# Weight splitter of a three-product fp32 block: a 60-unit ring of blocks becomes 15 equal cells, two kinds of VectorE additions become adding transfers, two preparations are spread out

## The chip, the cores and the metric

One core of one Trainium2 chip runs the whole kernel. The metric is the device time of one execution in microseconds; what is given is the median of several runs. TensorE, VectorE, ScalarE, GpSimd and SyncE are PE, DVE, ACT, POOL and SP in the profile's rows, and PEld is TensorE's loading of weights.

## The reference, cut to what matters

The input `x` has 256 tokens of 4096 channels. It is normalized, projected to 20480 channels, mixed in two branches, gated, merged and projected back; the residual is added, and a last RMSNorm follows.

```python
h = rmsnorm(x, norm_w)
proj = einsum('bsd,de->bse', h, w_in)              # 4096 -> 20480
u_p, z_p, u_c, b_c, c_c, z_c, g_logit = split(proj)
y_pool = causal_multiscale_pool(u_p, pool_w, pool_scale) * silu(z_p)   # windows 2, 4, 8, 16
y_conv = causal_gated_shortconv(u_c, b_c, c_c, conv_w, conv_b) * silu(z_c)
br = einsum('bsnc,ncd->bsnd', stack([y_pool, y_conv], 2), w_branch)    # 2 x (2048 -> 4096)
merged = sum(sigmoid(g_logit + gate_b) * br, axis=2)
x = x + einsum('bsd,de->bse', merged, w_out)       # 4096 -> 4096
return rmsnorm(x, final_norm_w)
```

## The kernel before

**Numbers.** Every fp32 operand of a product is split in two parts: ACT writes the rounded part (`act` to a float32r tile, the "high"), DVE writes what is left (`sub`, the "low"). A product is then three matmuls: high by high, high by low, low by high.

**Units and steps.** The work is a list of 32 units, each a block of 1024 output columns for all 256 tokens: 8 of the convolution (`cz`, `cb`, `cu`, `cc` for c = 0, 1), 4 of the pooling (`pz`, `pu`), 8 gate units (`g0_0`, `g1_0`, ... `g1_3`), 8 branch units (`b0_0` ... `b1_3`) and 4 output units (`o0` ... `o3`). A unit goes through its rows of weights in steps of 256 rows by 1024 columns (1 MB), 16 steps for 4096 rows and 8 for 2048. A string such as `EIGHT = "PSPSPSPSPSPSPSPS"` or `SIX4 = "PPPPSPSPSPSPSPSP"` gives the kind of each step. A **P** step multiplies directly: 24 matmuls of 128x512. An **S** step uses a seven-product scheme: 21 matmuls, but four sums of weight quarters must be formed first. In steps of both kinds TensorE streams the split weights and holds the split activations, which lie in `arena`.

**From weight to product.** SP loads a step's 1 MB into one of three `raw` buffers. For P, ACT writes highs of 2048 columns and DVE the lows. For S, ACT writes three quarters' highs, DVE forms four sums in `sums` (profile: `parts`), ACT writes their highs, DVE writes both kinds of lows. All go to `ring`, a tile of 60 units of 256 columns. `Ring.alloc` looks for a contiguous free block: 16 units for P, 12 for the three quarters of S, 16 for its sums, 16 or 8 for other uses. `Ring.release` gives a P block back in two halves, after 12 matmuls each, and an S block product by product.

**Order.** Every instruction is recorded in program order and engines follow that order. `pump()` lays preparation (`first()`, `rest()` of each step, in a queue `work`, first in, first out) up to four steps ahead of the step being multiplied, whenever the ring has room. `tick()` runs once per six matmuls and takes one entry from `queue`, a unit's epilogue; `gap(n)` puts n empty entries in it. `pop_fill()`, also once per tick, splits stored activations for the branch and output units. At a unit's end `combine(u)` adds the seven-product scheme's corner terms to the unit's result on DVE. The result stands in `E`, or in `Y` for some.

**Epilogues that matter here.** A gate unit adds a bias row to `E` on DVE: before its end POOL loads the row, broadcast to 128 partitions, into `Y`; then `add(E, E, ...)`, a sigmoid on ACT, a store. An output unit adds the residual rows of `x`, one token half at a time, through `Y`. `make_bands(c)` builds the banded matrices of the pooling on POOL and DVE, in one piece at the start of `cb0` and of `pu1`. In the first unit, `cz0`, `x_operand(j)` prepares x for step j just ahead of that step; for an S step that is two ACT scalings into `sa`, four DVE sums, an ACT high and a DVE low of 896 or 1024 columns.

Of the kernel before, what the change touches and what calls it, by code (L numbers as in the profile page):

```python
# [26 lines left out]
RING = 60  # L27
# [17 lines left out]
def hybrid_block(ctx: ExitStack, tc: tile.TileContext, x, xc, prm, rows_in, w_in, pool_w, w_branch, w_out, out):  # L45
# [28 lines left out]

    const = ctx.enter_context(tc.tile_pool(name="const", bufs=1))
# [8 lines left out]
    ring = sb("ring", [P, RING * KB], F32R)  # L84
# [67 lines left out]
    class Block:  # L152
        def __init__(self, at, parts):
            self.at, self.parts = at, parts

    class Ring:
        def __init__(self, size):
            self.size, self.head, self.live = size, 0, []

        def alloc(self, n, unit):  # L160
            for at in list(range(self.head, self.size - n + 1, 4)) + list(range(0, min(self.head, self.size - n + 1), 4)):
                if all(at >= a + m or a >= at + n for a, m in self.live):
                    parts = [(at + i, unit) for i in range(0, n, unit)]
                    self.live += parts
                    self.head = at + n
                    return Block(at, parts)
            return None

        def release(self, part):
            self.live.remove(part)  # L170

    rg = Ring(RING)

    def piece(block, off, n):
        o = (block.at + off) * KB
        return ring[:, o:o + n * KB]

    class Step:
        def __init__(self, unit, kind, src=None, op=None, **kw):
            self.unit, self.kind, self.src, self.op = unit, kind, src, op  # L180
            self.__dict__.update(kw)
            self.raw = None
            self.prepared = False
            self.pre = []

        def first(self):
            if self.kind == "P":
                def halves(block):
                    v = piece(block, 0, 16).rearrange("p (n a k c) -> p n a k c", n=2, a=2, k=2)
                    self.h, self.l, self.block = v[:, :, 0], v[:, :, 1], block  # L190
                    self.q = self.raw.rearrange("p (k n c) -> p n k c", k=2, n=2)
                    self.ks = (slice(0, 1), slice(1, 2)) if self is steps[0] else (slice(0, 2),)
                    for ks in self.ks:
                        act(self.h[:, :, ks], self.q[:, :, ks])

                return [((16, 8), None, halves)]
            if self.kind == "S":
                def direct(block):
                    self.q = self.raw.rearrange("p (i n) -> p i n", i=4)
                    self.bd = block  # L200
                    self.dh, self.dl = self.split(block, 3)
                    act(self.dh, self.q[:, 0:3])

                return [((12, 4), None, direct)]
            if self.kind == "M":
                def weights(block):
                    self.bw = block
                    self.h = piece(block, 0, 8).rearrange("p (k n) -> p k n", k=4)
                    self.l = piece(block, 8, 8).rearrange("p (k n) -> p k n", k=4)
                    self.q = self.raw.rearrange("p (k n) -> p k n", k=4)  # L210
                    act(self.h, self.q)

                return [((16, 16), None, weights)]
            return []

        def split(self, block, n):
            v = piece(block, 0, 4 * n).rearrange("p (i a n) -> p i a n", i=n, a=2)
            return v[:, :, 0], v[:, :, 1]

        def rest(self):  # L220
            if self.kind == "P":
                def lows(_):
                    for ks in self.ks:
                        sub(self.l[:, :, ks], self.q[:, :, ks], self.h[:, :, ks].bitcast(F32))

                return [(None, None, lows)]
            if self.kind == "S":
                def added(block):
                    q = self.q
                    self.bt = block  # L230
                    self.th, self.tl = self.split(block, 4)
                    add(sums[:, 0:2], q[:, 3:4].to_broadcast([P, 2, NH]), q[:, 1:3])
                    act(self.th[:, 0:2], sums[:, 0:2])
                    add(sums[:, 2], sums[:, 0], q[:, 2])
                    add(sums[:, 3], sums[:, 2], q[:, 0])
                    act(self.th[:, 2:4], sums[:, 2:4])
                    sub(self.dl, q[:, 0:3], self.dh.bitcast(F32))
                    sub(self.tl, sums, self.th.bitcast(F32))

                return [((16, 4), None, added)]  # L240
            if self.kind == "B":
                def parts(block):
                    self.block = block
                    self.h = piece(block, 0, 8).rearrange("p (t n) -> p t n", t=2)
                    self.l = piece(block, 8, 8).rearrange("p (t n) -> p t n", t=2)
                    act(self.h, E)
                    sub(self.l, E, self.h.bitcast(F32))

                return [((16, 16), lambda: self.unit.flags.get("base"), parts)]
            g = self.g  # L250
            e = E.rearrange("p a n -> p (a n)")[:, g * 1024:(g + 1) * 1024].rearrange("p (k t) -> p k t", k=4)

            def lows(_):
                sub(self.l, self.q, self.h.bitcast(F32))

            def pooled(block):
                self.ba = block
                self.ah = piece(block, 0, 4).rearrange("p (k t) -> p k t", k=4)
                self.al = piece(block, 4, 4).rearrange("p (k t) -> p k t", k=4)
                act(self.ah, e)  # L260
                sub(self.al, e, self.ah.bitcast(F32))

            return [(None, None, lows), ((8, 8), lambda: self.unit.flags.get(f"pooled{g}"), pooled)]

        def groups(self):
            gs = []
            if self is steps[0]:
                for k in (1, 0):
                    for i in range(3):
                        for n in range(2):  # L270
                            for t in range(2):
                                ah, al = self.op.standing(k, t)
                                h, l = self.h[:, 1 - n, 1 - k], self.l[:, 1 - n, 1 - k]
                                gs.append([("E", t, n), [((ah, h), (al, h), (ah, l))[i]], ()])
                gs[-1][2] = self.block.parts
            elif self.kind == "P":
                for n in reversed(self.halves):
                    for t in self.toks:
                        mm = []
                        for k in range(2):  # L280
                            ah, al = self.op.standing(k, t)
                            h, l = self.h[:, 1 - n, 1 - k], self.l[:, 1 - n, 1 - k]
                            mm += [(ah, h), (ah, l), (al, h)]
                        gs.append([("E", t, n), mm, ()])
                    if self.final:
                        gs[-1][2] = self.block.parts[1 - n:2 - n]
# [759 lines left out]
```

## Time and profile before

| | |
|---|---|
| median of 3 runs | 2499.02 us (2497.69 to 2499.75) |
| profiled execution: its own time | 2499.66 us |
| profiled execution: span of the trace | 2498.0 us |
| PE, DVE, ACT, POOL busy, share of the span | 96%, 87%, 57%, 3% |
| DMA, mean over the span | 220 GB/s |
| packets' share of the 16 DMA engines: SP's queue, POOL's queue | 53.8%, 7.1% |

The page first gives each engine's busy time, then the span in 40 slices, the DMA queues, the chain that ended last, and the costliest groups of instructions. A group's row has the line, the engine, the operation, output and inputs with shapes, the count, the busy time and the mean of one, and after the second bar the engine's idle time just before these instructions with what ended it. A timeline's row gives start and length in us and, in brackets, the idle time before it. A line such as L55 is a helper's (`tt`), so groups are told apart by their tiles.

### The profile page before, as it was taken

The numbers are of one execution on the slowest core, as the hardware profiler recorded it, in microseconds if no ns is written. First come the engines' busy times: TensorE is split into PE (matmuls) and PEld (weight loads), VectorE is DVE, ScalarE is ACT, GpSimd is POOL, SyncE is SP. The second block draws the span as 40 slices with busy tenths as digits, with TensorE's granted clock in tenths as the row PEclk, the third lists the DMA queues.
The fourth block names the chain that finished last, engine by engine and source line by source line (L and its number), as shares of the span: only waits on it lengthen the run. The fifth ranks groups of instructions, "written<-read, shape, count | busy, mean of one in ns | idle before, by whom it ended". The sixth has DMA issues, their size and how long they took to land.

```text
span 2498.0 us, 26581 instructions
## 1 busy us (share of the span) xinstructions
PE 2402.2 (96%) x10497; PEld 1963.3 (79%) x10497; DVE 2175.5 (87%) x1680; ACT 1417.8 (57%) x1294; POOL 66.5 (3%) x142
## 2 busy tenths in 40 slices
PE   8899999999999999999999999999999999999998
PEld 6677887888878888788777877887788877778886
DVE  7888899889988969869988998898888789899998
ACT  6655555555555546546555555555565555556555
POOL 0000000000000000000000000000000001000000
PEclk9899999999999999999999999999999999999999
DMA  8455466556556645546655665576767757557657
GB/s 305 167 202 202 165 239 212 194 201 227 196 198 217 218 174 203 203 176 219 238 210 188 232 240 206 186 260 219 248 230 271 267 216 276 210 185 279 229 212 274
DMA packets 82062, 549.15 MB, mean 220 GB/s; under 512 B 9360, under 2 KB 9360, under 8 KB 19856
## 3 DMA queue, kind: packets, MB, share of 16 engines
q1 hardware_dynamic: 68832, 484.47, 53.8%
q0 software_dynamic: 12672, 61.87, 7.1%
q8 instruction: 82, 1.34, 0.2%
q10 hardware_dynamic: 432, 1.11, 0.1%
q14 instruction: 44, 0.36, 0.0%
HBM read 518.05 MB, written 29.36 MB: 219 GB/s over the span
## 4 chain that ended last, share of the span: by engine, by line
PE 37%; DVE 13%; ACT 5%; issue 3%; DMA 0%; DVEq 0%; ACTq 0%
PE sums L857 29%; PE shared L857 7%; DVE ring L55 6%; ACT ring L52 3%; DVE parts L55 2%; DVE raw L55 1%; DVE E L55 1%; ACT E L52 1%; ACT raw L52 1%; DVE arena L55 1%; PE shared L541 0%; DMA raw<-in_w_out_dram 0%; DVE E L67 0%; ACT arena L52 0%; PE shared L388 0%
## 5 line engine op out<-in xcount | busy, mean ns | idle before, releaser
L857 PE MATMUL sums<-ring,arena 128*128 128x512 f32 x7827 | 1855.2, 394 | 69.9 <-DVE ring L55 51.3
L857 PEld LDWEIGHTS sums<-ring,arena 128*128 128x128 f32 x7827 | 1477.7, 190 | 401.4 <-DVE ring L55 72.2
L55 DVE TENSOR_TENSOR ring<-raw,ring 128x1536 fp32r<-128x1536 f32 (+2 forms) x453 | 929.8, 2053 | 188.1 <-ACT ring L52 173.2
L52 ACT ACTIVATE ring<-raw 128x1536 fp32r<-128x1536 f32 (+2 forms) x453 | 780.5, 1728 | 463.1 <-PE sums L857 296.4
L52 ACT ACTIVATE ring<-parts 128x1024 fp32r<-128x1024 f32 x390 | 407.0, 1060 | 349.4 <-DVE parts L55 325.8
L857 PE MATMUL shared<-ring,arena 128*128 128x512 f32 x2340 | 568.0, 391 | 0.6 <-DVE Y L67 0.4
L857 PEld LDWEIGHTS shared<-ring,arena 128*128 128x128 f32 x2340 | 439.9, 189 | 97.9 <-DVE ring L55 5.5
L55 DVE TENSOR_TENSOR ring<-parts,ring 128x2048 fp32r<-128x2048 f32 x195 | 445.9, 2287 | 47.2 <-ACT ring L52 42.8
L55 DVE TENSOR_TENSOR parts<-parts,raw 128x512 f32<-128x512 f32 x390 | 269.9, 692 | 13.3
L55 DVE TENSOR_TENSOR parts<-raw 128x1024 f32<-128x1024 f32 x195 | 237.7, 1219 | 2.8 <-DMA raw<-in_w_in_dram 1.3
L55 DVE TENSOR_TENSOR raw<-raw 128x512 f32<-128x512 f32 (+1 forms) x93 | 80.6, 867 | 2.1
L52 ACT ACTIVATE raw<-shared 128x512 f32<-128x512 f32 x124 | 68.5, 625 | 7.3 <-DVE ring L55 7.3
L52 ACT ACTIVATE E<-sums,rin 128x512 f32<-128x512 f32 x56 | 35.6, 689 | 51.6 <-PE sums L857 51.6
L55 DVE TENSOR_TENSOR E<-E,Y 128x2048 f32<-128x2048 f32 (+1 forms) x29 | 60.0, 2068 | 3.3 <-DMA Y<-p_d 3.0
L52 ACT ACTIVATE arena<-sa 128x512 fp32r<-128x512 f32 (+2 forms) x28 | 22.1, 790 | 54.1 <-DVE sa L55 48.5
L52 ACT ACTIVATE E<-sums 128x512 f32<-128x512 f32 x44 | 23.8, 598 | 36.7 <-PE sums L857 36.7
L55 DVE TENSOR_TENSOR arena<-sa,arena 128x512 fp32r<-128x512 f32 (+2 forms) x28 | 24.9, 890 | 19.6 <-ACT arena L52 19.5
L67 DVE SCALAR_TENSOR_TENSOR E<-raw,rin,E 128x1024 f32<-128x1024 f32 x28 | 34.7, 1282 | 0.6
L388 PE MATMUL shared<-ident,E 128*128 128x128 f32 x128 | 18.9, 282 | 10.6 <-DVE E L55 10.6
L388 PEld LDWEIGHTS shared<-ident,E 128*128 128x128 f32 x128 | 15.8, 146 | 14.9 <-issue 12.2
L55 DVE TENSOR_TENSOR E<-E,raw 128x2048 f32<-128x2048 f32 x11 | 25.2, 2292 | 0.4
L52 ACT ACTIVATE E<-E 128x2048 f32<-128x2048 f32 (+1 forms) x12 | 19.4, 1619 | 5.0 <-DVE E L55 5.0
(110 smaller groups left out, 387.9 us busy)
## 6 DMA issues: line engine op xcount, KB each, us to landing
raw<-in_w_in_dram SPq DMA_DIRECT2D x319, 1024.0 KB, 4.8
raw<-in_w_branch_dram SPq DMA_DIRECT2D x64, 1024.0 KB, 5.8
raw<-in_w_out_dram SPq DMA_DIRECT2D x64, 1024.0 KB, 4.9
gates_d<-E POOLq DMA_DIRECT2D x8, 1024.0 KB, 6.4
Y<-gates_d POOLq DMA_DIRECT2D x8, 1024.0 KB, 6.6
Y<-in_rows_dram POOLq DMA_DIRECT2D x12, 512.0 KB, 7.6
Y<-in_xc_dram SPq DMA_DIRECT2D x16, 256.0 KB, 5.7
E<-in_x_dram POOLq DMA_DIRECT2D x4, 1024.0 KB, 5.5
```

What stands on the lines that cost most here:

```text
L52: return pin(nc.scalar.activation(dst, src, func, **kw))
L55: return pin(nc.vector.tensor_tensor(out=dst, in0=a, in1=b, op=op))
L67: return pin(nc.vector.scalar_tensor_tensor(out=dst, in0=a, scalar=s, in1=b, op0=op0, op1=op1, **kw))
L388: pin(nc.tensor.transpose(shared(j)[:, i * T + t * P:i * T + (t + 1) * P], src[:, t, c:c + P], ident))
L857: pin(nc.tensor.matmul(ps, lhs, rhs, start=n == 0, stop=n == u.total[b] - 1))
```

## The change

The ring becomes 15 cells, each with a high and a low of 512 columns (the same memory). `alloc` takes the next n cells in circular order, which need not be contiguous; every cell is given back by itself. A run of cells that wraps round the end of the ring is written by two instructions in place of one. A P step's matmuls go by weight quarter (k outside n), so that a cell is free after six matmuls. An S step's sums and its direct lows are recorded before its four sum cells are asked for. Gate biases and the output's residual rows are added to `E` by POOL-issued transfers that accumulate, two per unit. The bands are built in timed pieces in the epilogues of `cu0` and `pz1`. x's sums have a second stage buffer, and their scaling, sums and lows are put in different steps. Some gaps and the sigmoid's and SiLU's pieces change.

```diff
-RING = 60
+CELLS = 15
+    def gather(dst, src):
+        return pin(nc.gpsimd.dma_start(dst, src, accum_op=ALU.add))
...
-    ring = sb("ring", [P, RING * KB], F32R)
+    ring = sb("ring", [P, CELLS, 2, NH], F32R)
...
+        def alloc(self, n):
+            cells = [(self.head + i) % CELLS for i in range(n)]
+            if self.live & set(cells):
+                return None
+            self.live |= set(cells)
+            self.head = (self.head + n) % CELLS
+            return cells
...
+    def highs(cells, src):
+        for i, c in runs(cells):
+            act(ring[:, c, 0], src[:, i])
+    def lows(cells, src):
+        for i, c in runs(cells):
+            sub(ring[:, c, 1], src[:, i], ring[:, c, 0].bitcast(F32))
...
             if self.kind == "S":
-                def added(block):
+                def added(_):
                     q = self.q
                     add(sums[:, 0:2], q[:, 3:4].to_broadcast([P, 2, NH]), q[:, 1:3])
-                    act(self.th[:, 0:2], sums[:, 0:2])
                     add(sums[:, 2], sums[:, 0], q[:, 2])
                     add(sums[:, 3], sums[:, 2], q[:, 0])
-                    act(self.th[:, 2:4], sums[:, 2:4])
-                    sub(self.dl, q[:, 0:3], self.dh.bitcast(F32))
-                    sub(self.tl, sums, self.th.bitcast(F32))
-                return [((16, 4), None, added)]
+                    lows(self.cells, q[:, 0:3])
+                def split(cells):
+                    self.sum_cells = cells
+                    highs(cells[0:2], sums[:, 0:2])
+                    highs(cells[2:4], sums[:, 2:4])
+                    lows(cells, sums)
+                return [(None, None, added)] + self.mid + [(4, None, split)]
...
             elif self.kind == "P":
-                for n in reversed(self.halves):
-                    for t in self.toks:
-                        for k in range(2):
...
-                    if self.final:
-                        gs[-1][2] = self.block.parts[1 - n:2 - n]
+                for k in (1, 0):
+                    for n in reversed(self.halves):
+                        cell = self.cells[2 * (1 - k) + 1 - n]
+                        for t in self.toks:
+                            ah, al = self.op.standing(k, t)
+                            gs.append([("E", t, n), [(ah, high(cell)), (ah, low(cell)), (al, high(cell))], ()])
+                        if self.final:
+                            gs[-1][2] = [cell]
...
     def gate_unit(n, c):
-        def start():
-            move(Y[:, 0], gate_b[n, None, c * NU:(c + 1) * NU].to_broadcast([P, NU]))
         def epi(u):
-            return gap(2) + [lambda: add(E, E, Y[:, 0:1].to_broadcast([P, 2, NU]))] + gap(3) + [
-                lambda: act(E, E, AF.Sigmoid), lambda: move(gates_d[n, c], E)]
+            def bias(t):
+                gather(E[:, t], gate_b[n, None, c * NU:(c + 1) * NU].to_broadcast([P, NU]))
+            return gap(1) + [lambda: bias(0), lambda: bias(1)] + gap(12) + [
+                lambda: act(E[:, 0], E[:, 0], AF.Sigmoid), None,
+                lambda: act(E[:, 1], E[:, 1], AF.Sigmoid), lambda: move(gates_d[n, c], E)]
...
-            return gap(1) + [lambda: mul(E, E, Y), lambda: move(Y, p_d[c])] + gap(7) + [
-                lambda: add(E, E, Y)] + gap(4) + pairs(transposes(E, copy)) + [
+            return gap(1) + [lambda: mul(E, E, Y), lambda: move(Y, p_d[c])] + gap(9) + [
+                lambda: add(E, E, Y)] + gap(5) + pairs(transposes(E, copy)) + [
...
             def row(t):
-                move(Y[:, 1], xrows[:, t, cs])
+                gather(E[:, t], xrows[:, t, cs])
...
-            return [lambda: row(0)] + gap(8) + [lambda: add(E[:, 0], E[:, 0], Y[:, 1]), lambda: row(1)] + gap(8) + [
-                lambda: add(E[:, 1], E[:, 1], Y[:, 1])] + gap(2) + [
+            return gap(1) + [lambda: row(0), lambda: row(1)] + gap(14) + [
                 lambda: square(0), lambda: square(1),
...
+        return [trailing] + gap(4) + [counts, leading] + gap(4) + [finished]      # band_items(c)
...
+    for j in range(16):
+        if j in staged:
+            steps[j - 1].pre.append(item(x_scale, j))
+            steps[j - 1].mid.append(item(x_sums, j))
+            steps[j].mid.append(item(x_rest, j))
         else:
-            parts_of(o, sa[:, 0:o.n])
+            before(j, x_direct, j)
...
-            make_bands(0)
-        if u.name == "pu1":
-            make_bands(1)
```

`x_scale` is the two ACT scalings, `x_sums` the four DVE sums with the ACT high, `x_rest` the DVE low; `x_direct` is the P steps' old path. `band_items(0)` stands in the epilogue of `cu0`, `band_items(1)` in that of `pz1`.

More of the change, by code (lines that the diff above doesn't have):

```diff
@@ L183, in __init__ @@
             self.prepared = False
-            self.pre = []
+            self.pre, self.mid = [], []
         def first(self):
[L187 to L218, printed above, removed]
+            if self.kind == "B":
+                return []
+            def rounded(cells):
+                self.q = self.raw.rearrange("p (i c) -> p i c", i=4)
+                self.cells = cells
+                if self is steps[0]:
+                    for i in (slice(0, 2), slice(2, 4)):
+                        highs(cells[i], self.q[:, i])
+                else:
+                    highs(cells, self.q[:, 0:len(cells)])
@@ L512, in band_sums, with finished @@
+        def finished():
+            for g in range(2):
+                w, q = WINDOWS[2 * c + g], scratch(g)
+                stt(edge[:, g], ident, -float(w), q[:, 0:P], ALU.mult, ALU.add)
+                stt(bands[:, g, 0:P], ident, cnt[:, g:g + 1], q[:, 0:P], ALU.mult, ALU.add)
+                pin(nc.vector.tensor_copy(bands[:, g, P:T], q[:, P:T]))
+        return [trailing] + gap(4) + [counts, leading] + gap(4) + [finished]
     def band_sums(st):
```

242 lines of the change are left out of this document (128 added, 114 removed).

## The prediction

> **What bounds the kernel now.** I read the page first, then the chain of waits, then windows cut at the unit boundaries, and the timeline of one unit of each kind.
>
> ```profile
> span 2498.0 us, 26581 instructions
> PE 2402.2 (96%) x10497; PEld 1963.3 (79%) x10497; DVE 2175.5 (87%) x1680; ACT 1417.8 (57%) x1294; POOL 66.5 (3%) x142
> ...
> PE 37%; DVE 13%; ACT 5%; issue 3%; DMA 0%; DVEq 0%; ACTq 0%
> ```
>
> PE is the bound, but DVE stands second and takes 13% of the chain: in places PE waits for split weights. How much, the pace tells. In an undisturbed stretch the chain has
>
> ```profile
> 1020.02 7.48 PE sums L857 x33
> ```
>
> so a 128x512 matmul costs 7.48/33 = 0.2267 us. A unit's window less its matmuls at this pace is what the unit loses. The windows (length, then busy time and count of each engine, then the granted clock), cut at unit boundaries:
>
> ```profile
> 7.20:117.40 110.20, 96.43 (x367) 74.54 (x368) 92.07 (x113) 70.31 (x85) 3.55 (x22) 0.92 0.66 243
> 117.40:208.30 90.90, 85.02 (x361) 69.48 (x360) 77.78 (x63) 50.45 (x42) 3.02 (x9) 0.94 0.53 185
> 992.00:1081.70 89.70, 83.95 (x361) 68.74 (x360) 75.21 (x61) 48.92 (x41) 3.02 (x9) 0.96 0.52 188
> 1181.20:1267.40 86.20, 82.66 (x362) 67.26 (x361) 77.03 (x55) 50.27 (x43) 1.07 (x2) 1.00 0.60 214
> 1267.40:1352.20 84.80, 82.69 (x362) 67.27 (x361) 76.75 (x54) 48.89 (x42) 1.07 (x2) 1.00 0.59 217
> 1606.50:1691.30 84.80, 82.68 (x361) 67.26 (x360) 74.31 (x51) 48.89 (x41) 2.14 (x4) 1.00 0.62 223
> 2000.60:2047.20 46.60, 43.51 (x184) 35.32 (x184) 39.85 (x27) 25.79 (x26) 1.08 (x2) 0.96 0.61 226
> 2237.00:2319.50 82.50, 81.85 (x361) 67.48 (x360) 78.29 (x55) 49.30 (x45) 2.11 (x4) 1.00 0.67 236
> ```
>
> In this order: `cz0` loses 110.2 - 367 x 0.2267 = 27.0, `cb0` 9.1, `pu1` 7.9, `g1_0` 4.1, `g0_1` 2.7, `g0_3` 3.0 (`g0_1` to `g0_3` are five units of one length), `b1_2` 4.9, and `o1` only 0.7. That last one sets what a unit with the same DVE combination, but no disturbance, loses. So the change has about 27 + 9 + 8 + 18 + 5 us of losses to work on.
>
> **The opening.** From 25 us on DVE works without a pause but for these waits, and PE waits for it. DVE's groups in 25 to 117.4, then in 117.4 to 141:
>
> ```profile
> L55 DVE TENSOR_TENSOR ring<-raw,ring 128x2048 fp32r<-128x2048 f32 x7 | 16.0, 2289 | 3.0 <-ACT ring L52 3.0
> ...
> L55 DVE TENSOR_TENSOR ring<-raw,ring 128x1536 fp32r<-128x1536 f32 x6 | 10.5, 1751 | 0.0
> L55 DVE TENSOR_TENSOR parts<-parts,raw 128x512 f32<-128x512 f32 x13 | 9.0, 692 | 0.4
> L55 DVE TENSOR_TENSOR parts<-raw 128x1024 f32<-128x1024 f32 x7 | 8.5, 1219 | 0.0
> ...
> L55 DVE TENSOR_TENSOR arena<-sa,arena 128x896 fp32r<-128x896 f32 x6 | 6.6, 1093 | 6.5 <-ACT arena L52 6.5
> ...
> L55 DVE TENSOR_TENSOR arena<-sa,arena 128x1024 fp32r<-128x1024 f32 x2 | 2.5, 1226 | 2.4 <-ACT arena L52 2.4
> ...
> L67 DVE SCALAR_TENSOR_TENSOR bands<-ident,cnt,sa 128x128 fp32r<-128x128 f32 x2 | 0.7, 352 | 0.1
> L67 DVE SCALAR_TENSOR_TENSOR edge<-ident,sa 128x128 fp32r<-128x128 f32 x2 | 0.6, 292 | 2.7 <-POOL sa L504 2.7
> L500 DVE TENSOR_REDUCE cnt<-sa 128x1 f32<-128x128 f32 x2 | 0.6, 282 | 0.0
> L510 DVE CAST bands<-sa 128x128 fp32r<-128x128 f32 x2 | 0.5, 270 | 0.0
> L507 DVE TENSOR_SCALAR cnt<-cnt 128x1 f32<-128x1 f32 x2 | 0.3, 147 | 0.0
> ```
>
> x's lows wait 6.5 + 2.4 = 8.9 us for ACT's high, because sums, high and low follow each other. After the change `added` or a P step's lows stand between (1.22 + 2 x 0.69 + 1.75 us or 2.29 us of DVE work against a wait of 8.9 / 8 = 1.1 us each): I take all 8.9. The bands leave this backlog: 2.7 us of wait for POOL and 0.7 + 0.6 + 0.6 + 0.5 + 0.3 = 2.7 us of work. Of the 3.0 us for ACT's ring writes I take 1.5: three of the fourth P step's four cells are still unused. Against it, of the first 32 allotments 4 wrap and split an instruction in two. The price of a split on DVE follows from the first and the fourth row above, 2 x 1.219 - 2.289 = 0.15 us; 4 are 0.6. **Opening: 8.9 + 5.4 + 1.5 - 0.6 = 15.2 us** (6 if the highs of x now queue behind weights' highs on ACT, 19 if PE's clock recovers too).
>
> Over the whole kernel the built program has 105 of 653 allotments that wrap, so 105 x 0.15 = 16 us more on DVE, and some 100 more instructions on ACT. Outside the stretches costed here this lies in DVE's idle time, 13% of the span by the page, so I cost it at nothing there; without that cover it is 16 us. [...]
>
> **The bands in `pu1`.** The same 5.4 us fall on DVE right after `combine`; the unit loses 7.9, against 0.7 in an undisturbed one. Moved into timed pieces, POOL's parts are done when DVE asks, and 2.7 us of DVE work remain in a unit where DVE is busy for 75.2 of some 82 us: I leave 2 us of loss there and add 0.5 in `cc0`. **5.4 us** (2 to 8).
>
> The granted clock speaks here too: 0.96 in `pu1`, 0.92 in `cz0`, but 1.00 in the gate units, whose waits are shorter. [...]
>
> **The gate units.** The start of `g0_1` on DVE, then PE and ACT:
>
> ```profile
> 1269.53 2.29 DVE L55 TENSOR_TENSOR ring<-parts,ring 128x2048 fp32r<-128x2048 f32 x1 [2.84 <-ACT ring L52]
> 1271.74 2.67 DVE L55 TENSOR_TENSOR raw<-raw 128x512 f32<-128x512 f32 x3
> 1274.44 2.48 DVE L67 SCALAR_TENSOR_TENSOR E<-raw,rin,E 128x1024 f32<-128x1024 f32 x2
> 1276.84 2.28 DVE L55 TENSOR_TENSOR ring<-raw,ring 128x2048 fp32r<-128x2048 f32 x1
> 1279.05 2.28 DVE L55 TENSOR_TENSOR E<-E,Y 128x2048 f32<-128x2048 f32 x1
> 1281.25 1.22 DVE L55 TENSOR_TENSOR parts<-raw 128x1024 f32<-128x1024 f32 x1
> ...
> 1279.18 5.73 PE L857 MATMUL sums<-ring,arena 128*128 128x512 f32 x24 [1.20 <-DVE ring L55]
> 1285.64 1.42 PE L857 MATMUL sums<-ring,arena 128*128 128x512 f32 x5 [0.73 <-DVE ring L55]
> ```
>
> PE first waits for the P lows that stand behind `combine`, then for the S lows that stand behind the bias addition of 2.28 us. In the new program's order on DVE the P lows come before `combine`, and the addition is gone. From the rows, after the unit's start at 1267.4: sum lows from 2.1 to 4.4 us, P lows to 6.7, `combine` (2.67 + 2.48) to 11.8, `added` (2.6) to 14.4, direct lows (1.75) to 16.2, where PE wants these 69 matmuls = 15.6 us after the start. So 0.6 to 0.7 us remain, what `o1` shows: 2.1 us less in each of five units, and one addition's 2.3 in `g1_0` and in `g1_3` each. **15.3 us** (8 to 20). What is late next is `combine` itself.
>
> **Branch and output units.** In `b1_2` PE waits for the P lows that stand behind `combine`:
>
> ```profile
> 2012.09 2.28 DVE L55 TENSOR_TENSOR ring<-raw,ring 128x2048 fp32r<-128x2048 f32 x1
> ...
> 2014.43 7.80 PE L857 MATMUL sums<-ring,arena 128*128 128x512 f32 x26 [3.09 <-DVE ring L55]
> ```
>
> Here too the new order has the P lows before `combine`: of 4.9 us I take **3.4** (0 to 5). In `b1_3` the order gains nothing. The residual additions leave units that lose 0.7: **1** (0 to 2).
>
> **Costs.** Three units end in a P step (`cz1`, `pz0`, `g1_3`). With k outside, a bank closes 9 matmuls before the next unit writes it, 2.04 us, where it was 18. From the rows
>
> ```profile
> L52 ACT ACTIVATE ring<-raw 128x2048 fp32r<-128x2048 f32 x256 | 490.6, 1917 | 119.9 <-PE sums L857 36.2 <-ACT ring L52 27.2 <-DMA raw<-in_w_branch_dram 16.3
> ...
> L52 ACT ACTIVATE E<-sums,rin 128x512 f32<-128x512 f32 x56 | 35.6, 689 | 51.6 <-PE sums L857 51.6
> ```
>
> a high of 1.92 just begun and an evacuation of 0.69 make 2.6, so about 1 us is lost in each: **-3** (0 to -8).
>
> The adding transfers are not in this trace. Nearest are
>
> ```profile
> raw<-in_w_in_dram SPq DMA_DIRECT2D x319, 1024.0 KB, 4.8
> ...
> gates_d<-E POOLq DMA_DIRECT2D x8, 1024.0 KB, 6.4
> Y<-in_rows_dram POOLq DMA_DIRECT2D x12, 512.0 KB, 7.6
> ```
>
> The plain broadcast of the same 512 KB lands after 7.6 us; a second one behind it adds perhaps half of a 1024 KB transfer, 2.5: 10 us for the pair. `E` is ready about 12 us after the unit's start. The sigmoid stands at the 16th tick, 16 x 6 x 0.2267 = 21.8 us, and ACT writes a step's highs a turn of 45 matmuls (10.2 us) before PE wants them, of which the high and the low take 4.2; with DVE's backlog I count 4 us of slack on ACT. The pair may thus take 21.8 - 12 + 4 = 13 us or so before weights come late; behind the waiting sigmoid ACT queues the highs of the coming steps, for which DVE and then PE wait. At the plain price it costs nothing, and I take that. It could not cost less than nothing, since the additions saved are already counted.
>
> **Sum.** 15.2 + 5.4 + 15.3 + 3.4 + 1 - 3 = 37.3 us. The profiled execution took 2499.66 us (1.66 around its span); the median of the runs is 0.64 below it. 2499.66 - 37.3 - 0.64 = 2461.7: **2462 us**. The terms' own ends, put together as independent, give 2454 to 2476.
>
> **Rivals.**
> *The adding transfers stall ACT (slower).* If a pair takes twice 10 us, the sigmoid, and the squares of the output units, wait 7 us in 8 + 3 units: 77 us, 2539. It decides from a pair of 13 + 37/11 = 16.4 us on. For it: no row shows what an accumulating transfer costs, and it must read `E` as well as the source. Against it: 13 ticks stand between the second transfer and the sigmoid.
> *The transfers land in time but delay the weights.* ACT already waits for loads:
>
> ```profile
> ACT ring L52 <- DMA raw<-in_w_in_dram: 40.1, 25, 4.5
> ...
> PE shared L388 <- DVE E L55: 10.6, 4, 2.7
> ```
>
> If a load's 4.8 us doubles while a pair is under way, I estimate 3 us of PE per unit, 33 in all: 2495. [...]
> *The opening does not do what it says.* If ACT's highs of x fall behind weights' highs, DVE waits as long in another place, and only the additions and the bands of `pu1` are gained: 2477.
> *More goes away.* If DVE's earlier work also ends the four waits of PE's transposes for `E` (10.6 us, second row above) and the rest of the opening's slow clock, another 22 us: 2440.
>
> **How the numbers follow.** Forecast 0.52, ACT stalled 0.12, weights delayed 0.12, opening unmoved 0.14, more 0.10. A measurement of this kernel can tell about 0.2% from no change, 5 us. Faster are the forecast, the opening, the more and a half of the delayed weights: 0.82. Same: 0.04 of the delayed weights. Slower: 0.14. The range reaches from 2440 to 2495; it leaves out the stalled ACT and a little beyond either end.
>
> **What would show it.** Right: DVE's waits for ACT's `arena` in the opening below 3 us; no wait of DVE for POOL; gate units of 82.5 to 83 us; the four transpose waits still there; pairs landing within 13 us and no wait of ACT's sigmoid for them. Wrong: ACT idle before the sigmoid on a DMA of `E`, more ACT idle on `raw`, evacuations of `E` on PE's list of waits at the ends of `cz1` and `pz0` beyond 1 us each.

## The result

The kernel after takes 2475.8 us (median of four runs, 2473.7 to 2477.9), the kernel before in the same series 2498.8 us: a ratio of 0.9908 (95% interval 0.9891 to 0.9925). It is faster by 23 us, inside the range, but 14 us short of the 2462 that were forecast. The profiled execution took 2475.7 us.

The head of the page after, and the windows of the units whose windows the prediction shows (`cz0`, `cb0`, `pu1`, `g1_0`, `g0_1`, `b1_2`, `o1`; length, busy time and count of PE, PEld, DVE, ACT and POOL, granted clock, DMA share, GB/s):

```profile
span 2473.9 us, 26884 instructions
PE 2390.4 (97%) x10497; PEld 1964.9 (79%) x10497; DVE 2155.7 (87%) x1769; ACT 1445.6 (58%) x1401; POOL 86.3 (3%) x150
...
7.10:114.60 107.50, 93.59 (x366) 72.53 (x367) 91.64 (x114) 69.18 (x85) 2.14 (x3) 0.95 0.65 249
114.60:198.20 83.60, 82.08 (x362) 67.43 (x361) 75.48 (x59) 52.02 (x48) 0.00 (x0) 1.00 0.57 202
...
1000.10:1081.70 81.60, 81.60 (x361) 67.56 (x360) 74.54 (x62) 48.51 (x43) 4.92 (x6) 1.00 0.59 206
1181.20:1262.90 81.70, 81.70 (x362) 67.53 (x361) 74.83 (x59) 51.70 (x48) 2.33 (x3) 1.00 0.70 237
1262.90:1344.60 81.70, 81.70 (x361) 67.48 (x360) 74.58 (x56) 50.04 (x46) 2.25 (x3) 1.00 0.66 227
...
1984.60:2026.20 41.60, 41.60 (x185) 34.34 (x185) 35.53 (x22) 23.24 (x22) 1.07 (x2) 1.00 0.67 260
2216.80:2298.40 81.60, 81.60 (x362) 67.59 (x361) 76.56 (x59) 50.23 (x50) 2.86 (x4) 1.00 0.70 239
```

From the third row on PE is busy for the whole window: 360 matmuls at the pace of 0.2267 us are 81.6 us (183 in `b1_2` are 41.5), and next to nothing is lost; `cb0`, the second row, still loses 2.0 us. The span should therefore have fallen by more than 24 us. Five units ate the rest: `cu0`, `cz1` (88.8 to 93.5 us), `cu1`, `pz0` (89.3 to 92.6) and `g1_3`. The windows of `cu0`, `cu1` and `g1_3`, first before and then after:

```profile
208.30:296.80 88.50, 85.84 (x380) 70.83 (x379) 75.80 (x54) 47.41 (x44) 0.57 (x1) 0.98 0.57 202
...
551.10:638.10 87.00, 84.34 (x381) 69.62 (x379) 75.54 (x54) 47.41 (x44) 0.56 (x1) 1.00 0.57 206
...
1691.30:1781.70 90.40, 84.56 (x367) 68.04 (x365) 78.25 (x70) 52.66 (x50) 6.99 (x13) 1.00 0.68 236
```

```profile
198.20:292.30 94.10, 86.84 (x381) 71.62 (x380) 75.80 (x58) 50.20 (x49) 4.12 (x23) 0.95 0.53 190
...
549.70:644.50 94.80, 86.84 (x381) 71.65 (x380) 75.67 (x59) 50.65 (x49) 0.56 (x1) 0.95 0.52 193
...
1671.50:1769.40 97.90, 85.37 (x367) 67.88 (x365) 81.94 (x80) 55.61 (x58) 9.30 (x16) 0.97 0.71 242
```

The five are longer by 5.6, 4.7, 7.8, 3.3 and 7.5 us, 28.9 in all. So the other units gained 53 us, against 37 forecast for everything. (Where a unit's loss is given below, it is the time from its first matmul to the next unit's first, less its own matmuls at 0.2267 us. The windows hold a matmul or two of the neighbours, so the prediction's losses are up to 0.5 us smaller. Losses and waits are those of one profiled execution; where it lies more than 2 us from the median of its runs, that is said.) The list of waits after names both causes:

```profile
PE shared L386 <- DVE E L55: 25.9, 5, 8.0
...
PE sums L900 <- ACT E L52: 14.3, 2, 10.2
```

The first row is the wait for `E` of the transposes, which PE does early in `cu0`, `cz1`, `cu1` and `pz0` on the result of the unit before (10.6 us before, 25.9 now, all but 0.5 of it in these four units). The second is the wait of a unit's first matmuls for the evacuation of the unit before, ACT's copy of its result out of the banks into `E`: 8.7 us before, 14.3 now, 10.2 us of it once, at the end of `g1_3`.

Why the transposes wait longer is seen in the timelines of DVE and PE at the start of `cu0`, first before (it begins at 208.3 us), then after (198.2 us):

```profile
210.78 2.29 DVE L55 TENSOR_TENSOR ring<-raw,ring 128x2048 fp32r<-128x2048 f32 x1 [2.21 <-ACT ring L52]
212.99 2.67 DVE L55 TENSOR_TENSOR raw<-raw 128x512 f32<-128x512 f32 x3
215.69 2.48 DVE L67 SCALAR_TENSOR_TENSOR E<-raw,rin,E 128x1024 f32<-128x1024 f32 x2
218.21 2.29 DVE L55 TENSOR_TENSOR E<-E,Y 128x2048 f32<-128x2048 f32 x1
...
220.64 1.09 PE L388 MATMUL shared<-ident,E 128*128 128x128 f32 x4 [2.66 <-DVE E L55]
```

```profile
203.22 1.22 DVE L55 TENSOR_TENSOR parts<-raw 128x1024 f32<-128x1024 f32 x1 [1.05 <-DMA raw<-in_w_in_dram]
204.48 1.42 DVE L55 TENSOR_TENSOR parts<-parts,raw 128x512 f32<-128x512 f32 x2
205.81 1.75 DVE L55 TENSOR_TENSOR ring<-raw,ring 128x1536 fp32r<-128x1536 f32 x1
207.48 2.67 DVE L55 TENSOR_TENSOR raw<-raw 128x512 f32<-128x512 f32 x3
210.19 2.48 DVE L67 SCALAR_TENSOR_TENSOR E<-raw,rin,E 128x1024 f32<-128x1024 f32 x2
212.70 2.29 DVE L55 TENSOR_TENSOR E<-E,Y 128x2048 f32<-128x2048 f32 x1
...
215.14 1.09 PE L386 MATMUL shared<-ident,E 128*128 128x128 f32 x4 [7.26 <-DVE E L55]
```

The first three rows of the kernel after are `added` for the unit's first S step, which stands only fourth in the text of `cu0`: PE will want it 72 matmuls, 16 us, after the unit's start. It no longer waits for sum cells, so it is recorded in the last pump of the unit before, ahead of `combine` (rows four and five). With its wait for a load it is 5.4 us; the transposes come 16.9 us after the unit's start instead of 12.3, and their wait is 4.6 us longer. In `cz1` and `pz0` no S step is near; there one more P step's lows (2.28 us), whose cells are free earlier now, have got between `combine` and the multiplication, and the wait is 5.4 and 4.7 us.

### The profile page after: what moved, and what is told of

Its sections match the earlier page's. It is cut to its first block, busy times and chain, and to the rows that moved or that the text cites. A ratio compares the mean times of both kernels' runs of the same rounds, so it can differ in the third digit from the quotient of the medians.

```text
span 2473.9 us, 26884 instructions
## 1 busy us (share of the span) xinstructions
PE 2390.4 (97%) x10497; PEld 1964.9 (79%) x10497; DVE 2155.7 (87%) x1769; ACT 1445.6 (58%) x1401; POOL 86.3 (3%) x150
## 4 chain that ended last, share of the span: by engine, by line
PE 82%; DVE 10%; ACT 4%; issue 2%; DMA 2%; SPq 0%; DVEq 0%; POOL 0%; ACTq 0%; POOLq 0%
PE sums L900 61%; PE shared L900 19%; DVE ring L55 4%; ACT ring L52 3%; DVE parts L55 2%; PE shared L560 1%; PE shared L386 1%; DVE raw L55 1%; DMA raw<-in_w_in_dram 1%; DVE E L55 1%; DVE sa L55 1%; DVE arena L55 1%; ACT raw L52 0%; DVE E L67 0%; ACT E L52 0%
## 5 line engine op out<-in xcount | busy, mean ns | idle before, releaser
L900 PE MATMUL sums<-ring,arena 128*128 128x512 f32 x7827 | 1841.1, 393 | 33.6 <-ACT E L52 14.3
L55 DVE TENSOR_TENSOR ring<-raw,ring 128x2048 fp32r<-128x2048 f32 (+3 forms) x518 | 935.0, 1815 | 190.9 <-ACT ring L52 190.2
L52 ACT ACTIVATE ring<-raw 128x2048 fp32r<-128x2048 f32 (+3 forms) x518 | 787.6, 1535 | 436.5 <-PE sums L900 264.3
L52 ACT ACTIVATE ring<-parts 128x1024 fp32r<-128x1024 f32 (+1 forms) x418 | 412.6, 1002 | 330.6 <-DVE parts L55 296.1
L55 DVE TENSOR_TENSOR ring<-parts,ring 128x2048 fp32r<-128x2048 f32 (+3 forms) x233 | 449.2, 1940 | 55.6 <-ACT ring L52 55.0
L386 PE MATMUL shared<-ident,E 128*128 128x128 f32 x128 | 20.8, 301 | 25.9 <-DVE E L55 25.9
L55 DVE TENSOR_TENSOR E<-E,Y 128x2048 f32<-128x2048 f32 x15 | 34.3, 2286 | 0.1
L52 ACT ACTIVATE Y<-shared 128x512 f32<-128x512 f32 x24 | 13.4, 596 | 32.7 <-PE shared L386 30.2
L55 DVE TENSOR_TENSOR arena<-sa,arena 128x512 fp32r<-128x512 f32 (+2 forms) x28 | 24.9, 888 | 8.7 <-ACT arena L52 8.7
L52 ACT ACTIVATE E<-sums 128x512 f32<-128x512 f32 x44 | 25.1, 595 | 11.6 <-PE sums L900 10.4
L76 POOL DMA_DIRECT2D E<-in_rows_dram x16 | 13.9, 867 | 441.8 <-DVE E L67 439.6
```

Source lines behind the costliest of these rows:

```text
L52: return pin(nc.scalar.activation(dst, src, func, **kw))
L55: return pin(nc.vector.tensor_tensor(out=dst, in0=a, in1=b, op=op))
L76: return pin(nc.gpsimd.dma_start(dst, src, accum_op=ALU.add))
L386: pin(nc.tensor.transpose(shared(j)[:, i * T + t * P:i * T + (t + 1) * P], src[:, t, c:c + P], ident))
L900: pin(nc.tensor.matmul(ps, lhs, rhs, start=n == 0, stop=n == u.total[b] - 1))
```

## The experiments

### One part undone at a time

**Sums formed only with their cells.** The work items of an S step become one again:

```diff
-                return [(None, None, added)] + self.mid + [(4, None, split)]
+                return [(4, None, added)] + self.mid      # added forms, rounds and subtracts the sums
```

> Undoes one part: an S step's sums are formed only when its four sum cells are free; the ring of equal cells, the adding transfers and the spread pieces stay. Theory (the early sums help the gate units but get ahead of `combine` where a unit starts with three P steps): PE's waits of the transposes for E at the starts of cu0 and cu1 fall from 8.1 and 7.4 us to about 3 each, all transposes together from 25.9 to 16 us; the gate units lose 1 to 2 us each again; 2476 to 2482 us. Rival (the cells given back one by one bring the gate units' gain by themselves, the early sums only harm): transposes at 16 us, gate units unchanged at 81.7 us, 2466 us. Rival (the transposes wait for another reason): transposes still about 26 us and 2485 us or more.

2468.2 us (2464.7 to 2470.1; ratio 0.9878, 0.9863 to 0.9893). The list of waits has

```profile
PE shared L384 <- DVE E L55: 16.3, 5, 5.4
```

as both the first and the second theory said. `cu0` loses 3.9 instead of 11.8 us, `cu1` 6.8 instead of 12.5, and the gate units stay at 81.6 to 81.8 us: the second theory. Forming sums early brought nothing to the gate units, and costs this kernel 7.6 us. What it does bring is small: without it the opening (`cz0` and `cb0`) takes 1.5 us more, `g1_3` 2.1, the last three units 1.4.

**DVE's additions back.** `gate_unit` and `out_unit` load into `Y` and call `add` as in the kernel before; the sigmoid keeps its tick.

> Undoes one part: the gates' biases and the residual are loaded into Y and added by DVE as in the kernel before; the sigmoid stands where it stands in the kernel after. Theory (DVE's 2.3 us stand between combine and weights that PE waits for): eight gate units take 2 us more each and the output units 1 in all, 2492 us. Rival (with the P step's lows ahead of combine the additions lie in DVE's idle time): within 5 us of 2476. Rival (the adding transfers cost something hidden): under 2471 us.

2493.8 us (ratio 0.9982, 0.9973 to 0.9992), 18 us slower than the kernel after, as the theory had it. Where it falls is seen at the start of `g0_1` (1267.5 us) on DVE, behind `combine`, and on PE:

```profile
1278.85 2.29 DVE L55 TENSOR_TENSOR E<-E,Y 128x2048 f32<-128x2048 f32 x1
1281.06 1.22 DVE L55 TENSOR_TENSOR parts<-raw 128x1024 f32<-128x1024 f32 x1
1282.31 1.42 DVE L55 TENSOR_TENSOR parts<-parts,raw 128x512 f32<-128x512 f32 x2
1283.65 1.82 DVE L55 TENSOR_TENSOR ring<-raw,ring 128x1024 fp32r<-128x1024 f32 x2
...
1284.92 1.45 PE L901 MATMUL sums<-ring,arena 128*128 128x512 f32 x5 [1.42 <-DVE ring L55]
```

PE waits for the direct lows, which stand behind the addition. The six gate units that start PS lose 2.2 to 4.0 us, against 3.2 to 4.6 before and 0 to 0.2 after: 18.9 in all, against 20.5 and 0.7. So the P step's lows ahead of `combine` alone bring little; on top of the new ring the adding transfers bring nearly all of it.

**Bands in one go**, at the starts of `cb0` and `pu1`:

> Undoes one part: the two sets of bands are made in one go, at the starts of cb0 and pu1 as in the kernel before, not in timed pieces in cu0 and pz1. Theory (DVE's 2.7 us of wait for POOL and 2.7 us of work come at a point where PE waits for DVE): 5.4 us in each of two places, 2487 us, with DVE waits for POOL back at 2.7 us or so each. Rival (the new order leaves DVE enough lead there): under 2480 us.

2488.0 us (ratio 0.9958, 0.9943 to 0.9973): 12.2 us slower than after. `cb0` loses 7.9 instead of 2.0 us and `pu1` 5.0 instead of 0.0. DVE's wait for POOL is 2.7 us in four pieces, half of what was expected, yet the two units lose 10.9 us more, the theory's sum. That DVE's work there delays weights as much as its wait does is the reading left; no run parts the two.

**x's operands in one piece:**

> Undoes one part: each of x's operands is scaled, summed, rounded and subtracted in one piece ahead of its step, as in the kernel before. Prediction's term (all 8.9 us of DVE's waits for ACT's arena come back): 2485 us. Theory after the result (part of the 8.9 us only moved to DVE's waits for ACT's ring): 2480 us, DVE's waits for ACT's arena back near 9 us and those for ACT's ring in the opening smaller by 4 to 6. Rival (the pieces bring nothing): within 2 us of 2476.

2475.2 us (ratio 0.9907, 0.9890 to 0.9923): no difference, the rival. DVE's waits in the opening, from 25 us to the end of `cz0`, first of this kernel and then of the kernel after:

```profile
DVE arena L55 <- ACT arena L52: 8.8, 8, 1.2
DVE ring L55 <- ACT ring L52: 1.4, 2, 0.9
```

```profile
DVE ring L55 <- ACT ring L52: 10.1, 7, 3.1
```

8.8 + 1.4 = 10.2 us against 10.1: the pieces move DVE's wait from x's highs to the weights' highs and shorten it by nothing. `cz0` and `cb0` together are 1.8 us longer without them, in an execution that took 3 us more than the median.

**The ring alone,** all four undoings at once:

> The kernel after with the four other parts undone together: sums with their cells, DVE additions in place of the adding transfers, bands at once, x's operands in one piece. What is left is the ring of 15 equal cells given back one by one, and the order of matmuls in a P step. Theory (the parts add: the single undoings gave -8, +18, +12 and -1 us against 2476): 2497 us, no gain by itself, though the adding transfers lost 26 us without it. Rival (the earlier lows of a P step gain by themselves, and the parts overlap): 2485 us or less. Rival (the ring costs by itself, since its cells wrap and units end in k-outer P steps, and the other parts only pay for it): 2505 us or more.

2489.3 us (2487.4 to 2493.1; ratio 0.9966, 0.9953 to 0.9978). The ring, with its order of matmuls and the moved ticks, gains 8 us by itself; the sum of single undoings missed by that. That the parts meet in the same units is the likely reason, and not tested. `b1_2` loses 0.0 instead of 5.1 us and the opening 3.2 us less, while `cz1`, `cu1`, `pz0` and `g1_3` together lose 14.7 us more than in the kernel before (the profiled execution took 2493.1 us).

### The adding transfers without the ring

The kernel before, with `gather` and the epilogues of gate and output units from the kernel after:

> The kernel before with one part of the change: biases and residual by adding transfers into E, with the sigmoid and the squares at the ticks that they have in the kernel after. Theory (in the gate units the 2.3 us addition is the whole loss, and the order of a P step's lows and `combine` brings nothing): the six gate units that start PS lose 0.7 to 1 us instead of 3.2 to 4.6, all in all 15 us less, 2484 us. Rival (the prediction's: 2.1 us of the additions come only together with the P step's lows ahead of combine): the gate units lose 2.5 us, 2494 us.

2524.3 us (2522.7 to 2530.7; ratio 1.0109, 1.0092 to 1.0126): 26 us **slower** than the kernel before, which neither theory had. The profiled execution was the longest of the four, 2530.7 us. In it the six gate units that start PS lose 3.8 to 6.5 us instead of 3.2 to 4.6, though DVE no longer adds the bias there, and `o1`, `o2` and `o3` lose 7.5, 7.1 and 7.9 us instead of 0.9, 1.0 and 1.8. In `o1` (2249.5 to 2338.5 us), on ACT and PE:

```profile
2270.34 1.91 ACT L52 ACTIVATE ring<-raw 128x2048 fp32r<-128x2048 f32 x1 [5.96 <-PE shared L860]
2272.64 1.48 ACT L52 ACTIVATE ring<-raw 128x1536 fp32r<-128x1536 f32 x1 [0.38 <-DMA raw<-in_w_out_dram]
...
2272.31 0.50 PE L860 MATMUL sums<-ring,arena 128*128 128x512 f32 x1 [1.30 <-ACT ring L52]
2274.64 9.64 PE L860 MATMUL sums<-ring,arena 128*128 128x512 f32 x29 [1.82 <-DVE ring L55]
```

and the DMA issues of 2259 to 2266 us, with the median from issue to landing, and then those of 2272 to 2285 us, when the pair had landed:

```profile
raw<-in_w_out_dram SPq DMA_DIRECT2D x3, 1024.0 KB, 10.1
E<-in_x_dram POOLq DMA_DIRECT2D x2, 512.0 KB, 8.0
```

```profile
raw<-in_w_out_dram SPq DMA_DIRECT2D x3, 1024.0 KB, 4.8
```

A load that meets the pair takes 10.1 us instead of 4.8. The wait of 5.96 us is put down to PE, whose group ended at about the same time; but the load of that step was issued at 2260.67 and landed at 2270.24, 0.1 us before the high began. That is the rival "delay the weights" of the prediction, alive in the old ring. The 4.8 and 10.1 us show slower loads; how the pair slows them no run shows. In the kernel after the pair does the same to the loads beside it (`o1`, 2227 to 2237 us):

```profile
raw<-in_w_out_dram SPq DMA_DIRECT2D x3, 1024.0 KB, 7.1
E<-in_x_dram POOLq DMA_DIRECT2D x2, 512.0 KB, 10.0
```

but there PE does not stop: in `o1` it is busy for 81.60 of 81.60 us. In the old ring the next three loads were issued at 2260.67 to 2264.93, the first of them 12 us after the load before, and all behind the pair (2259.00); in the kernel after three had been issued between 2215.34 and 2227.50, ahead of it (2228.03). The runs with sums formed only with their cells, with bands in one go and with x's operands in one piece have the pair too, and lose 0.0 to 0.2 us in the six gate units; so none of these parts is what covers it. What is left is the ring with its order of matmuls, whose cells and loads come earlier: it is the cover that makes the adding transfers free. (The sigmoid and the squares stand later in this run than in the kernel before; that they cost nothing in the old ring was not tested by itself.)

### The two new losses taken away

**`combine` first.** Right behind `combine` comes the multiplication, and no `added` of a unit is recorded before the `combine` of the unit ahead:

```diff
+            mul(E, E, Y)                       # in epi, at once behind combine
-            return gap(1) + [lambda: mul(E, E, Y)] + gap(4) + transposes(E, copy) + ...
+            return gap(6) + transposes(E, copy) + ...
...
-                return [(None, None, added)] + self.mid + ...
+                return [(None, combined, added)] + self.mid + ...   # combined: combine(units[v - 1]) is recorded
```

> Moves only DVE's order: where a unit's epilogue ends in transposes, the multiplication of E by Y is recorded at once behind `combine`, and the early sums of a following unit wait until `combine` is recorded; the transposes stay at their tick. Theory (the early sums and one more P step's lows stand between the unit's end and E): in cu0 and cu1 the wait of the transposes falls by the 4.4 us of the sums and their direct lows and in cz1 and pz0 by the 2.3 us of the lows, 25.9 to about 12 us in all; 2462 us. Rival (E is late because of the corner copies or the evacuations): the waits stay above 20 us and the time above 2472 us.

2568.4 us (ratio 1.0279, 1.0264 to 1.0294). A miss, by the edit's reach. The transposes did what the theory said,

```profile
PE shared L390 <- DVE E L55: 11.7, 5, 3.3
```

and `cu0`, `cz1`, `cu1` and `pz0` lose 22.7 us instead of 44.6. But the six gate units that start PS lose 6.4 to 7.3 us instead of 0.0 to 0.2, and most other such units about as much. There the held `added` is that of the second step, the work list behind it is held too, and lows that stood ahead of `combine` now stand behind it, so that PE stops at the unit's first S step (`g0_1`, begun at 1275.0 us):

```profile
1285.30 1.84 PE L906 MATMUL sums<-ring,arena 128*128 128x512 f32 x5 [4.51 <-DVE ring L55]
```

**The transposes two ticks later,** `gap(6)` made `gap(8)` on top of that:

> As the run with `combine` first, and besides it the four transposes stand two ticks (12 matmuls, 2.7 us) later. Theory (the waits that are left come from a transpose that is placed before E can be ready, 12 us after the unit's start): under 3 us of waits for E in all, 2452 us. Rival (the banks are then late for the first S step, or DVE's lows become the next wait): as the run with `combine` first, 2462 us, with waits of PE for ring or shared in their place.

2564.8 us (ratio 1.0263, 1.0248 to 1.0278), and in an execution of 2567.6 us

```profile
PE shared L390 <- DVE E L55: 1.6, 3, 0.5
```

The waits of transposes are gone as the theory had them; the loss in the other units stayed. In `cz1` and `pz0` PE now waits 2.1 and 2.7 us a little later, for DVE's next work on `Y`.

**Held in `cu0` and `cu1` alone:** the same, with `combined` asked only of units named `cu`:

> The transposes two ticks later and the multiplication at once behind `combine` as before; the early sums wait for `combine` only in cu0 and cu1, where transposes follow. Theory (the loss of 7 us in each unit that starts PS came from holding the early sums there, and the four units with transposes gained what was expected): those units lose 0 to 0.2 us again, and cu0, cu1, cz1 and pz0 together 17 us instead of 45; 2449 us. Rival (the units that start PS lost for another reason, the multiplication or the later transposes): above 2476 us.

2450.3 us (2448.6 to 2452.3; ratio 0.9808, 0.9791 to 0.9824), 1 us from the theory's number and 25 us faster than the kernel after. `cu0`, `cz1`, `cu1` and `pz0`:

```profile
198.50:282.60 84.10, 84.10 (x380) 69.67 (x379) 75.40 (x58) 49.81 (x49) 6.09 (x23) 1.00 0.61 213
364.70:454.70 90.00, 87.13 (x383) 71.04 (x381) 80.87 (x73) 50.04 (x53) 2.05 (x3) 0.98 0.60 212
536.50:621.40 84.90, 84.37 (x381) 69.64 (x380) 75.08 (x59) 50.11 (x49) 0.55 (x1) 1.00 0.61 215
703.10:792.80 89.70, 86.88 (x383) 70.99 (x381) 80.23 (x70) 49.89 (x50) 2.01 (x3) 0.98 0.60 212
```

`cu0` has no wait at all. `cz1` and `pz0` lose 7.1 and 6.8 us, a little more than before the change, with the wait for `Y` in them; the four units lose 18.3 us together. The six gate units that start PS lose 0.0 to 0.2 us again.

**The end of `g1_3`.** ACT's timeline there, in the kernel after, and PE's next matmuls; PE's last matmul of the unit ended at 1759.2:

```profile
1762.63 1.93 ACT L52 ACTIVATE ring<-raw 128x2048 fp32r<-128x2048 f32 x1
1767.85 0.95 ACT L52 ACTIVATE arena<-sb 128x896 fp32r<-128x896 f32 x1 [3.29 <-DVE sb L55]
1768.70 2.40 ACT L52 ACTIVATE E<-sums,rin 128x512 f32<-128x512 f32 x4
...
1769.43 2.93 PE L900 MATMUL sums<-ring,arena 128*128 128x512 f32 x6 [10.25 <-ACT E L52]
```

The four evacuations stand behind a fill of a later operand, which waits for DVE's sums. Two edits, each alone: the last P step of a unit by output halves (`n` outside, `k` inside, as before), and no fill in `g1_3`'s last two steps.

> Changes only the order of matmuls in the last step of cz1, pz0 and g1_3: the output half outside and k inside, as in the kernel before, so that the first bank closes 18 matmuls before the unit's end. Theory (k outside makes the four evacuations of E queue behind ACT's other work at the end): g1_3's loss falls from 15.0 to the 7.4 us it had before, cz1 and pz0 by 1 us each, 2467 us. Rival (the fill of a later operand, whose high waits for DVE's sums ahead of the evacuations, makes g1_3's wait): g1_3's wait for E stays near 10 us and the time within 2 us of 2476.

> Changes only when operands are filled: in the last two steps of g1_3 no operand of a later unit is filled or fetched. Theory of the fill (its high waits 3.3 us for DVE's sums, ahead of the evacuations, and with its other highs and lows takes 5 us of ACT and DVE): g1_3's wait for E falls from 10.3 to about 4 us, 2469 us, unless the fill is then missing in b0_0. Rival (the late closing of the banks makes the wait): it stays above 8 us, and the time within 2 us of 2476.

By halves: 2474.4 us (ratio 0.9901, 0.9886 to 0.9916), not told apart from the kernel after. `g1_3` lost 8.4 instead of 15.0 us, near the theory's 7.4, but `b0_0` 6.6 instead of 2.0 and `o0` 11.0 instead of 9.7; `cz1` and `pz0` gained only 0.2 and 0.1. So the time came out as the rival had it. Without fills: 2472.8 us (ratio 0.9895, 0.9878 to 0.9911), not clearly told apart from the kernel after either; in an execution of 2469.8 us the wait fell from 10.25 to 5.49 us, `g1_3` lost 10.4 and `b0_0` 2.4. So the late evacuation has both causes. By halves, most of what `g1_3` gains is lost again in `b0_0`; without fills little of it is.

**All together,** with x's sums behind the split where an S step precedes:

> As the run with the early sums held in cu0 and cu1 alone; besides it nothing is filled in g1_3's last two steps, the last step of cz1, pz0 and g1_3 is taken by output halves, and in the opening the sums for an operand that follows an S step come behind that step's split. Theory (late evacuation of g1_3 has two causes that add up): PE's wait for E at g1_3's end under 2 us and g1_3 and b0_0 together 12 us of loss instead of 17; opening 3 us less (two waits of DVE for ACT's ring of 3.1 us go); 2441 us. Rival (both only uncover the fills' work in b0_0, and the opening is bound by the sum of DVE's work): 2449 us.

2444.9 us (2444.6 to 2445.3; ratio 0.9787, 0.9772 to 0.9801): faster than both kernels, 53 us below before and 31 below after, and halfway between the theory's 2441 and the rival's 2449. `g1_3` loses 8.6 and `b0_0` 3.0 us, 11.6 together as expected, though PE's wait for `E` there is still 3.6 us and not under 2. The 3 us expected of the opening did not come (24.9 us lost in `cz0`, 25.1 without the edit): DVE's waits for ACT's ring fell to 7.4 us, and one of 3.2 us for `root`'s square root came in their place.

## Why the prediction was right and where it failed

**Right in sign and, for the gains, in mechanism.** DVE's work between a unit's end and the weights PE wants was the loss; taking it away brought back the units' length. The number is another matter: 2476 us is what the rival of the unmoved opening gave (2477), and it is not what happened, for the opening gained 10 us. The 14 us by which the forecast missed are what is left, to the rounding, of 13 us more gained and 26 us more lost than the sum had. The gate units came out at 81.6 to 81.8 us instead of 82.5 to 83; in the six that start PS some 20 us were gained, for 5 x 2.1 + 2.3 = 12.8 in the sum (with the 2.3 us for `g1_3` its terms make 15.1, not the 15.3 that stand there). The term was too small because I left in each what `o1` lost, and that went too (in `o1` as well), and because I credited `g1_0` with 2.3 of its 4.6. The P step's lows, given there as a cause, are a small one, as the run with DVE's additions shows. Likewise `pu1` gave 8.1 for 5.4, `b1_2` 5.1 for 3.4, and `o1` to `o3` 3.5 for 1.

**The four transposes: the step that failed.** "The four transpose waits still there", costed at no change, because their rows were 10.6 us of an old loss. They are 25.9 us now, and with the slower matmuls that follow (in `cu1` the first six of 128x512 behind the wait took 2.91 us, 1.63 before), the four units are 21.4 us longer. The order on DVE was in hand: for the gate units the prediction walked it from row to row, but not for the units that start with three or four P steps, where the same early recording brings nothing (the need is 16 us away) and delays `E`, which a transpose 36 matmuls into the unit wants. The wait has a fixed place in PE's order, so each microsecond that DVE is later is at least a microsecond of PE: in `cu0` the wait grew by 4.6 us and the unit by 5.6.

**The end of `g1_3`: mis-sized.** 1 us was taken for it, 3 for the three units that end in a P step, 8 at the far end; `g1_3` alone lost 7.5 us more, though the addition saved is already in that. The estimate of one high and one evacuation forgot that fills of later operands run at this point, and that their highs wait for DVE. In `cz1` and `pz0`, which have no fills, the order by halves is worth 0.1 to 0.2 us, less than the 1 us taken.

**The opening: 10.0 us for 15.2.** The bands' 5.4 are 6.4 by the run with bands at once. The 8.9 us of waits for ACT's arena are gone, as said, but the waits for ACT's ring, expected to fall by 1.5, rose by 7.1 to 10.1 us. A wait of DVE for ACT was moved, not removed: ACT itself waits for DVE's sums of x before it can round them (31.4 us in eight waits from 25 us to the end of `cz0`, 23.7 before), and the weights' highs stand behind that. This was the rival "the opening does not do what it says" in its outcome, with the order the other way round: x's highs hold up the weights'. It is true of x's pieces, not of the bands.

**The adding transfers: free, as forecast.** By the page's DMA issues the gates' sixteen land 10.0 us after their issue in the median; in `g0_1` the pair takes 12.6 us from the first issue to the second landing, for 10 estimated and 13 allowed. The eleven pairs take 12.5 to 14.5 us, four of them over 13, and still no sigmoid or square waits for one. One sign named as wrong did come: ACT's idle time on loads of `raw` rose from 99.7 to 113.1 us, but the six gate units that start PS and `o1` to `o3` lose 0.0 to 0.2 us all the same. But the reason given was not enough. I named the ticks before the sigmoid as the cover; the cover that decides is the lead of the loads, and without it they cost 26 us. The rival of delayed weights (33 us) needs only the old ring to come true: 2524 us is 30 and 40 us above what the two theories of that run had without a delay.

The errors went both ways: 53 us gained against 40 in the sum's gains, 29 lost against 3. Of the granted clock the rows of the prediction show only that lower clocks stood beside longer waits: 0.92 in `cz0` and 0.96 in `pu1`, whose longest waits of PE are 2.75 and 3.03 us, against 1.00 in `g1_0` and `g0_1` with 1.61 and 1.20.

## What to carry to other kernels

Work that is made ready early takes its place in an engine's order: ask for each unit what it gets ahead of, and whether that is wanted sooner. An edit that lets work run ahead needs a look at every place with a fixed consumer behind it (here the transposes and the last evacuations), not only at the place it is meant for. And a transfer that is free in one kernel may cost in another (the pairs: 0.0 to 0.2 us lost in each of nine units with the new ring, 26 us in all with the old one): its price lay here in the loads it delayed, 10.1 us instead of 4.8, and those are free only as far as the ring has lead.

## What was not expected of the hardware

Two adding transfers of 512 KB in flight made 1024 KB loads take 7.1 to 10.1 us instead of 4.8. And slower matmuls stood behind some of PE's waits, so that the unit lost more than the wait: `cu1` holds the same matmuls before and after, and PE was busy for 84.34 us at a granted clock of 1.00 where its transposes waited 2.66 us, but for 86.84 us at 0.95 where they waited 8.0; the first six matmuls of 128x512 behind the wait took 1.63 and 2.91 us. The length of the wait alone does not part the cases: in `cu0` before the transposes waited the same 2.66 us, and those six took 2.80 us, with 85.84 us busy at 0.98 in its row above. What decides it no run here shows.
